# Evacuations and a triangular inverse dealt anew among ScalarE, VectorE and GpSimd in a chunked delta-rule scan

## The chip, the core and the metric

One core of a Trainium2 chip runs the whole program. The metric is the device time of one execution in microseconds. Engines are written as in the profile: PE (TensorE matmul), PEld (its weight loads), DVE (VectorE), ACT (ScalarE), POOL (GpSimd) and SP (the queue that issues most DMAs).

## The reference, cut to what matters

One inference step of a two-layer trunk of width 1024 over 128 prompt tokens and 512 latent tokens. Layer 0 mixes tokens with a gated MLP, layer 1 with RWKV-7: two scans, forward and backward, over a 64x64 state for each of 16 heads. The edit is in the scans.

```python
def _wkv_scan(s0, r, decay, k, v, kk, a, reverse):
    def step(s, inp):
        r_t, w_t, k_t, v_t, kk_t, a_t = inp
        sa = jnp.einsum('bhij,bhj->bhi', s, -kk_t)
        s = (s * w_t[:, :, None, :]
             + sa[..., None] * (kk_t * a_t)[:, :, None, :]
             + v_t[..., None] * k_t[:, :, None, :])
        return s, jnp.einsum('bhij,bhj->bhi', s, r_t)
    ...
for d in range(N_DIR):
    ...
    s_fin, y_d = _wkv_scan(s0[:, d], r, decay, k_d, v, kk, a, reverse=(d == 1))
    y = y + y_d
```

Prompt and latent tokens run through the same weights; the latent scan starts from a cached state, the prompt scan from zero, and the prompt's final states are an output.

## The kernel before

The scans are done in chunks of 64 tokens: 2 chunks of prompt and 8 of latents, ten in all. Within a chunk the delta rule needs the inverse of a unit triangular 64x64 matrix for each head. So the work has four parts, for eight groups g = 0 to 7 (four pairs of head pairs, p = g // 2, in two directions, d = g % 2):

- The inverse of a group (`inv_start`, `inv_prep`, `inv_sub`). A DVE transpose (L836) lays out the two 32x32 diagonal blocks of all chunks and heads as LA, 128 partitions with one small matrix each. Then come 31 steps of forward substitution, each an outer product (L843) and a subtraction (L845) on LX. Step s works on rows s+1 to 31 and columns 0 to s. In the kernel before, POOL does columns 0 to 10 (`CS = 11`), and DVE the columns from 11 on in the steps s = 11 to 30, in instructions that `spread` deals out over the slots of the schedule. The inverse of group 0 runs earlier, under the projections, and wholly on POOL.
- `merges`: two DVE transposes of LX (L978, L981), 80 small matmuls with their ACT evacuations (L1002, L1019) that build the off-diagonal blocks, and four copies of diagonal blocks into TT, the finished inverse (L1024, DVE).
- `Front`: for each of ten units of a group, three products into PSUM. `p1` gives the score matrices B (a masked half, L927 on DVE, and a plain half, L929 on ACT), `wt` gives WT (L944, DVE), `wp` multiplies by TT and gives WP (L958, ACT).
- `chain`: ten dependent steps a group, one for each chunk, both head pairs (ti) in each. `part1` multiplies the state in RZ by WP into PSUM za; both heads' halves are evacuated, negated, into RZ (head 0 by ACT at L1066, head 1 by DVE at L1067). `part2` adds the products with B into PSUM sy; the state rows are evacuated with a scale into the next chunk's RZ (head 0 by DVE at L1088, head 1 by ACT at L1086), the output rows into Y (L1091 on ACT for d = 0, added on DVE at L1093 for d = 1). PSUM holds one za, and one sy for each ti, so the next step's sy has to wait for these evacuations.

Two tables say where in the program each part is written: `FA` gives the slots of the units of a group (20 slots a group, two a step), `MG` and `MGS` those of the merges. The inverse of group j is started in slot 7 of group j-2, and merged in group j-1. The order of instructions on each engine is then set when the program is built: a list scheduler with its own costs puts each instruction into its engine's queue as soon as its inputs are ready by those costs, chain instructions first (`tc.high_priority(30)`). On the chip each queue runs strictly in that order. SBUF space for the four pieces LA, LX and the two transposes (`piece`) is used again from inverse to inverse.

```python
def inv_start(d):
    LA, LX = piece(), piece()
    inv_prep(d, LA, LX)
    for s in range(31):
        inv_sub(nc.gpsimd, inv[:, 4416:4648], LA, LX, s, 0, min(s + 1, CS))
    return LX, [lambda s=s: inv_sub(vec, inv[:, 4648:4880], LA, LX, s, CS, s + 1) for s in range(CS, 31)]
```

Of the kernel before, what the change touches and what calls it, by code (L numbers as in the profile page):

```python
# [7 lines left out]
F32 = mybir.dt.float32  # L8
# [7 lines left out]
P = 128  # L16
# [12 lines left out]
def tile_trunk(ctx: ExitStack, tc: tile.TileContext, a: dict):  # L29
# [782 lines left out]

    def rwkv_core(dr, PC, bon, nn, ATs, go):
        with ExitStack() as es:
            CS = 11
            NR, NK = 10, 4

            xw = Pool(hctx, "cxw", {"w": 1}, side="right")
# [41 lines left out]
            while not go:  # L860
                yield
            xk = Pool(hctx, "cx", {"x": 1})
            cp = Pool(es, "cc", {"T": 4, "K": NK, "B": 8, "WT": 3, "WP": 7, "R": NR, "TT": 2, "b": 9})
            ea, ef = ExitStack(), ExitStack()
            cl = ap = None

# [20 lines left out]
                vec.memset(x, 0.0)  # L887
            turn_ = [0]

            mT = cp.tile([P, 2, 2, 64], F32, "WT", "mT")  # L890
            vec.memset(mT, 1.0)
            for d in range(2):
                for h in range(2):
                    a0 = 64 * h
                    vec.tensor_copy(mT[a0:a0 + 64, d, 1 - h], masks[a0:a0 + 64, 1 - d, 0])

            class Front:
                def __init__(self, g):
# [19 lines left out]
                def p1(self, i):  # L918
                    u = self.buf[self.units[i]]
                    R, Tt = u[0], u[3]  # L920
                    B = cp.tile([P, 2, 4, 64], F32, "B", "B")
                    ps = pf.tile([P, 2, 4, 64], F32, "p", "p1")
                    for e in range(2):
                        for x, j in ((R[:, :, e], 3 * e), (ident.rearrange("p (h c) -> p h c", h=2), 1 + e)):
                            for m in range(2):
                                pe.matmul(ps[64 * m:64 * m + 64, :, j], Tt[:, 2 * e + m], x, start=True, stop=True)  # L926
                    vec.tensor_tensor(out=B[:, :, 0:4:3], in0=ps[:, :, 0:4:3], op=ALU.mult,  # L927
                                      in1=masks[:, self.d, 1].unsqueeze(1).unsqueeze(1).to_broadcast([P, 2, 2, 64]))
                    act.copy(B[:, :, 1:3], ps[:, :, 1:3])  # L929
                    u[4] = B  # L930


# [15 lines left out]
                def wp(self, i):  # L948
                    ti, q = self.units[i]
                    u = self.buf[ti, q]  # L950
                    W = u[3]
                    ps = pf.tile([P, 2, 4, 64], F32, "p", "wpps")
                    for e in range(2):
                        for j in range(2):
                            pe.matmul(ps[64 * j:64 * j + 64, :, e], W[:, e, j],  # L955
                                      TTs[self.d][:, 10 * ti + 2 * q + e], start=True, stop=True)
                    WP = cp.tile([P, 2, 2, 64], F32, "WP", "WP")
                    act.copy(WP, ps[:, :, 0:2])  # L958
                    u[2] = WP

            def load_AT(g):
# [5 lines left out]
            def inv_start(d):  # L967
                LA, LX = piece(), piece()
                inv_prep(d, LA, LX)
                for s in range(31):  # L970
                    inv_sub(nc.gpsimd, inv[:, 4416:4648], LA, LX, s, 0, min(s + 1, CS))
                return LX, [lambda s=s: inv_sub(vec, inv[:, 4648:4880], LA, LX, s, CS, s + 1) for s in range(CS, 31)]

            def merges(d, LX):
                AT, TT = ATs[d], TTs[d]
# [45 lines left out]

                def diag(h, b):
                    p0 = 64 * h + 32 * b
                    vec.tensor_copy(TT[p0:p0 + 32, :, h, 32 * b:32 * b + 32],  # L1024
                                    XDT[p0:p0 + 32].rearrange("p t u -> p u t")[:, U0[d]:U0[d] + 20])

                for ti in range(2):
# [22 lines left out]
            def part1(d, fr, RZ, c, ti, upd):  # L1050
                q, e = divmod(c, 2)
                with HP():
                    R, _, WP, _, _ = fr.buf[ti, q]
                    za = pp.tile([P, 8, 64], F32, "za", "za")[:, 0]
                    sy = pp.tile([P, 8, 64], F32, f"sy{ti}", "sy")[:, 0:2]
                    for h in range(2):
                        a0 = 64 * h
                        pe.matmul(za[a0:a0 + 64], WP[:, h, e], RZ[:, ti, h, c], start=True, stop=True)  # L1058
                    s0, y0 = 64 * (1 - e), 64 * e
                    for h in range(2):  # L1060
                        a0 = 64 * h
                        if upd:
                            pe.matmul(sy[s0:s0 + 64, h], ident[:, a0:a0 + 64], RZ[:, ti, h, c],
                                      start=h == 0, stop=False)
                        pe.matmul(sy[y0:y0 + 64, h], R[:, h, e], RZ[:, ti, h, c], start=h == 0, stop=False)
                    act.activation(out=RZ[0:64, ti, 0, c], in_=za[0:64], func=AF.Copy, scale=-1.0)  # L1066
                    vec.tensor_scalar(out=RZ[64:128, ti, 1, c], in0=za[64:128], scalar1=-1.0, scalar2=None, op0=ALU.mult)  # L1067
                return sy

            def part2(d, p, fr, RZ, c, nxt, ti, sy, Y, so):  # L1070
                q, e = divmod(c, 2)
                with HP():
                    B = fr.buf[ti, q][4]
                    s0, y0 = 64 * (1 - e), 64 * e
                    upd = nxt is not None or c < 2
                    for h in range(2):
                        if upd:
                            pe.matmul(sy[s0:s0 + 64, h], B[:, h, 1 + e], RZ[:, ti, h, c], start=False, stop=h == 1)  # L1078
                        pe.matmul(sy[y0:y0 + 64, h], B[:, h, 3 * e], RZ[:, ti, h, c], start=False, stop=h == 1)  # L1079
                    if upd:  # L1080
                        for h in range(2):
                            a0 = 64 * h
                            dst = RZ[a0:a0 + 64, ti, h, nxt] if nxt is not None else so[a0:a0 + 64, ti]
                            pc = PC[s0:s0 + 64, d, 2 * p + ti, h, q:q + 1]
                            if h:
                                act.activation(out=dst, in_=sy[s0:s0 + 64, h], func=AF.Copy, scale=pc)  # L1086
                            else:
                                vec.tensor_scalar(out=dst, in0=sy[s0:s0 + 64, h], scalar1=pc, scalar2=None, op0=ALU.mult)  # L1088
                    Yc = Y[y0:y0 + 64, q]
                    if d == 0:  # L1090
                        act.copy(Yc, sy[y0:y0 + 64])  # L1091
                    else:
                        vec.tensor_tensor(out=Yc, in0=Yc, in1=sy[y0:y0 + 64], op=ALU.add)  # L1093
                    if nxt is None and c < 2 and ti:
                        nc.sync.dma_start(out=a["sT"][:, 2 * p:2 * p + 2, d], in_=so)
# [123 lines left out]

            class Tail:  # L1220
                def __init__(self):
                    self.rings = {"x": (3, []), "r": (3, []), "o": (3, []), "s": (2, [])}
                    self.x, self.stored = None, []
                    self.first = self.early()

# [200 lines left out]
            FA = (-8, -6, -4, -2, 0, 2, 4, 6, 8, 10)  # L1426
            MG = (4, 5, 7, 8, 9, 10, 11)
            LAP = 7
            DV0, DV1 = (7, 24)
            ADA = (0, 1, 3, 7, 9, 10, 11, 14, 15, 19)  # L1430
            AG = 2
            FW = (1, 3, 1, 1, 1, 1, 1, 1, 1, 1, 1, 1, 1, 1, 1, 1, 1, 1, 1, 1)
# [5 lines left out]
            GE = vec  # L1438
            STQ = nc.scalar
            posts = []  # L1440
            MGS = {0: (5, 6, 8, 9, 10, 11, 12), 1: (6, 7, 9, 10, 11, 11, 12)}
            ZL = 4
            DVI = (0, 5)
            sched = {}

            def at(k, f):
                sched.setdefault(k, []).append(f)

            def spread(fs, a, b):
                for i, f in enumerate(fs):  # L1450
                    at(a + i * (b - a) // len(fs), f)

            spread(lx[1][1], *DVI)
            for g in range(8):
                for i in range(10):
                    k, f = 20 * g + FA[i], fr[g]
                    for k0, x in ((k - 6, f.load), (k - 3, f.p1), (k - 2, f.wt), (k, f.wp)):
                        at(max(k0, -1), lambda i=i, x=x: x(i))
            for x in sched.pop(-1):
                x()  # L1460
            for j in range(2, 8):
                k0 = 20 * (j - 2) + (ZL if j == 2 else 0)

                def start(j=j, k0=k0):
                    lx.append(inv_start(j % 2))
                    spread(lx[j][1], k0 + DV0, min(k0 + DV1, 20 * j - 20 + MGS.get(j - 1, MG)[0]))

                at(k0 + LAP - 4, lambda j=j: load_AT(j))
                at(k0 + LAP, start)
# [14 lines left out]
            for g in range(8):  # L1484
# [4 lines left out]
                if g < 7:  # L1489
                    ms = {}  # L1490

                    def merge(g=g):
                        if g not in ms:
                            ms[g] = merges((g + 1) % 2, lx[g + 1][0])
                        adv(ms[g])

                    for x in MGS.get(g, MG):
                        at(20 * g + x, merge)
# [205 lines left out]
```

## Time and profile before

| | |
|---|---|
| median of 3 runs | 2150.9 us (2149.31 to 2154.84) |
| profiled execution | 2151.84 us, span 2150.1 us |
| PE busy | 2001.1 us, 93% |
| DVE busy | 1175.1 us, 55% |
| ACT busy | 753.8 us, 35% |
| POOL busy | 383.3 us, 18% |
| the scans | from about 1075 to 1610 us of the span |

The spans of PE are modelled and its matmuls are pipelined, so its 93% is not a measure of how full it is. In the lines of groups, the last column is the time for which an engine sat idle just before an instruction of the group, and what ended it. In a table of stretches, the columns behind an engine's busy time are the granted TensorE clock, the DMA share and GB/s.

### The profile page before, as it was taken

Reading aid. Unit: us, or ns where it says so; the run is one execution under the profiler, and the core shown is the slowest. Engines: PE = TensorE matmul, PEld = TensorE weight load, DVE = VectorE, ACT = ScalarE, POOL = GpSimd, SP = SyncE. Lnnn points to the kernel's source line nnn. Section 1 sums busy time; section 2 is a strip of 40 time slices with the busy share of each in tenths; the row PEclk is TensorE's granted clock in tenths of the full one; section 3 lists DMA queues with packets and bytes.
Section 4 is the critical chain, followed back from the end, with each engine's and each line's share of the span. In section 5 each row is a group of like instructions: output and inputs, shape, how many; then the busy total and the mean of one; then the engine's idle time right before and its main releaser. Section 6 shows DMA issues by size and latency. Waiting matters only on the chain.

```text
span 2150.1 us, 43942 instructions
## 1 busy us (share of the span) xinstructions
PE 2001.1 (93%) x18294; PEld 1763.8 (82%) x18294; DVE 1175.1 (55%) x2231; ACT 753.8 (35%) x1505; POOL 383.3 (18%) x681
## 2 busy tenths in 40 slices
PE   6999999999999798989888998888998999999997
PEld 5767889999999587878677776766765899999997
DVE  5435643333333796767688877757455633333334
ACT  5323531313132264655444433432422522222231
POOL 0000000000000301588367435414000000000000
PEclk9999999999999799989889998987999999999998
DMA  8554352222222033666442344442440222222221
GB/s 279 203 193 161 114 177 70 79 75 73 79 71 79 19 119 126 191 197 198 140 117 74 114 142 123 141 130 66 135 131 30 79 79 78 70 79 73 75 69 50
DMA packets 149670, 241.78 MB, mean 112 GB/s; under 512 B 28128, under 2 KB 98400, under 8 KB 149344
## 3 DMA queue, kind: packets, MB, share of 16 engines
q1 hardware_dynamic: 149040, 238.52, 34.8%
q8 instruction: 144, 2.36, 0.5%
q14 instruction: 54, 0.44, 0.1%
q10 hardware_dynamic: 432, 0.46, 0.1%
HBM read 197.63 MB, written 38.67 MB: 110 GB/s over the span
## 4 chain that ended last, share of the span: by engine, by line
PE 76%; POOL 8%; DVE 8%; issue 3%; ACT 3%; DMA 2%; SPq 0%; POOLq 0%; DVEq 0%; ACTq 0%
PE fmps L114 46%; PE zps L310 5%; POOL inv L845 3%; POOL inv L843 3%; PE vps L754 2%; PE p L926 2%; PE rps L114 2%; PE wops L1271 2%; PE wops L1371 1%; PE adaps L122 1%; PE adaps L1193 1%; PE sy L1078 1%; PE wtps L942 1%; PE l1ps L507 1%; PE wpps L955 1%
## 5 line engine op out<-in xcount | busy, mean ns | idle before, releaser
L114 PE MATMUL fmps<-ahi,whi 128*128 128x256 f32 (+1 forms) x2272 | 534.6, 310 | 4.9 <-ACT ahi L100 3.1
L114 PE MATMUL fmps<-alo,whi 128*128 128x256 f32 (+1 forms) x2272 | 533.7, 309 | 1.3 <-DVE alo L101 1.3
L114 PE MATMUL fmps<-ahi,wlo 128*128 128x256 f32 (+1 forms) x2272 | 533.8, 309 | 0.0
L114 PEld LDWEIGHTS fmps<-ahi,whi 128*128 128x128 f32 x2272 | 414.4, 188 | 11.0 <-ACT ahi L100 5.5
L114 PEld LDWEIGHTS fmps<-alo,whi 128*128 128x128 f32 x2272 | 415.1, 188 | 2.1 <-DVE alo L101 1.8
L114 PEld LDWEIGHTS fmps<-ahi,wlo 128*128 128x128 f32 x2272 | 415.2, 188 | 1.0 <-issue 0.8
L88 ACT CAST whi<-wraw 128x1024 fp32r<-128x1024 f32 x174 | 182.5, 1050 | 633.5 <-PE fmps L114 538.2
L89 DVE TENSOR_TENSOR wlo<-wraw,whi 128x1024 fp32r<-128x1024 f32 x174 | 216.3, 1244 | 273.2 <-ACT whi L88 273.0
L283 DVE SCALAR_TENSOR_TENSOR x<-fmps,mod,x 128x128 f32<-128x128 f32 (+2 forms) x153 | 74.5, 527 | 305.4 <-PE fmps L114 305.4
L491 POOL TENSOR_TENSOR xx<-h 128x254 f32<-128x254 f32 (+1 forms) x16 | 12.0, 751 | 724.7 <-DVE h L210 710.0
L843 POOL TENSOR_TENSOR inv<-inv 128x220 f32<-128x220 f32 (+29 forms) x217 | 100.3, 462 | 165.7 <-DVE inv L836 149.2
L845 POOL TENSOR_TENSOR inv<-inv 128x220 f32<-128x220 f32 (+29 forms) x217 | 101.0, 466 | 17.0
L1078 PE MATMUL sy<-RZ,B 128*64 128x64 f32 x576 | 79.8, 244 | 14.1 <-ACT RZ L1066 7.7
L1079 PE MATMUL sy<-RZ,B 128*64 128x64 f32 x640 | 87.6, 244 | 1.1 <-DVE RZ L1067 0.8
L926 PE MATMUL p<-cst,Tt 128*64 128x128 f32 x640 | 87.4, 291 | 0.0
L926 PE MATMUL p<-R,Tt 128*64 128x128 f32 x640 | 85.8, 297 | 0.2 <-DMA R<-dR 0.2
L1078 PEld LDWEIGHTS sy<-RZ,B 128*64 128x64 f32 x576 | 56.3, 146 | 35.6 <-ACT RZ L1066 14.8
L1058 PE MATMUL za<-RZ,WP 128*64 128x64 f32 x640 | 67.1, 245 | 16.0 <-DVE RZ L1088 8.1
L1066 ACT ACTIVATE RZ<-za 64x64 f32<-64x64 f32 x160 | 34.8, 217 | 126.3 <-PE za L1058 69.2
L955 PE MATMUL wpps<-TT,WT 128*64 128x128 f32 x640 | 68.2, 290 | 11.4 <-ACT B L929 7.0
L101 DVE TENSOR_TENSOR alo<-rsq,ahi 128x640 fp32r<-128x640 f32 (+2 forms) x69 | 53.6, 777 | 45.6 <-ACT ahi L100 45.3
L942 PE MATMUL wtps<-cst,K 128*64 128x64 f32 x640 | 70.2, 235 | 8.9 <-DVE WT L944 4.5
(282 smaller groups left out, 3690.2 us busy)
## 6 DMA issues: line engine op xcount, KB each, us to landing
wraw<-w SPq DMA_DIRECT2D x126, 512.0 KB, 3.5
wraw<-ada SPq DMA_DIRECT2D x64, 512.0 KB, 5.0
adaw<-adac SPq DMA_DIRECT2D x32, 512.0 KB, 3.7
dT<-IT SPq DMA_DIRECT2D x16, 640.0 KB, 3.9
Tt<-dT SPq DMA_DIRECT2D x80, 128.0 KB, 2.7
wraw<-w_in SPq DMA_DIRECT2D x16, 512.0 KB, 5.1
dR<-KR SPq DMA_DIRECT2D x16, 320.0 KB, 3.3
dT<-KR SPq DMA_DIRECT2D x16, 320.0 KB, 3.0
```

The source lines that it names most:

```text
L88: act.copy(hi[:, :n], r[:, :n])
L89: vec.tensor_tensor(out=lo[:, :n], in0=r[:, :n], in1=hi[:, :n], op=ALU.subtract)
L114: pe.matmul(ps[:, PS0 + t0:PS0 + t1], w, x[:, t0:t1], start=start, stop=stop)
L283: vec.scalar_tensor_tensor(out=X[n][:, t0:t1], in0=ps[:, t0 - r[0]:t1 - r[0]], scalar=mod[l][:, which, n, g:g + 1], in1=X[n][:, t0:t1], op ...
L310: pe.matmul(pss[i], x[:, i * P:(i + 1) * P], w[:, kq * 512:(kq + 1) * 512], start=(k == 0 and j == 0), stop=(k == KT - 1 and j == 2))
L843: eng.tensor_tensor(out=tv, in0=LA[:, s + 1:32, s:s + 1].to_broadcast([P, n, m]), in1=LX[:, s:s + 1, c0:c1].to_broadcast([P, n, m]), op=AL ...
L845: eng.tensor_tensor(out=LX[:, s + 1:32, c0:c1], in0=LX[:, s + 1:32, c0:c1], in1=tv, op=ALU.subtract)
L926: pe.matmul(ps[64 * m:64 * m + 64, :, j], Tt[:, 2 * e + m], x, start=True, stop=True)
L942: pe.matmul(ps[a0:a0 + 64, e, j], K[:, h, e], x, start=True, stop=True)
L955: pe.matmul(ps[64 * j:64 * j + 64, :, e], W[:, e, j], TTs[self.d][:, 10 * ti + 2 * q + e], start=True, stop=True)
L1078: pe.matmul(sy[s0:s0 + 64, h], B[:, h, 1 + e], RZ[:, ti, h, c], start=False, stop=h == 1)
L1079: pe.matmul(sy[y0:y0 + 64, h], B[:, h, 3 * e], RZ[:, ti, h, c], start=False, stop=h == 1)
```

## The change

It deals the work of the scans out anew, and moves the program's slots for group 1.

- POOL does all columns of the inverse (`inv_sub(..., 0, s + 1)`); the DVE pieces and their `spread` go.
- The four diagonal copies of a merge go from DVE to POOL (L1027).
- ACT does all four evacuations that the chain waits for: both halves of za (L1071) and both of the state (L1089).
- DVE does all those of the products: B in one instruction of 512 columns with a mask mB that holds ones in the plain half (L932), WT (L947), WP (L961), and Y for both directions (L1092, L1094).
- The slots of group 1's units come from tables of their own (L1, P1, W1, F1), later than before, its merges move from slots 5 to 12 to slots 11 to 17, and inverse 2 starts three slots later (`ZL`).
- SBUF: mB is new, mT gets a place of its own, and the pools b and the tail's ring o lose a buffer each.

```diff
-                    vec.tensor_tensor(out=B[:, :, 0:4:3], in0=ps[:, :, 0:4:3], op=ALU.mult,
-                                      in1=masks[:, self.d, 1].unsqueeze(1).unsqueeze(1).to_broadcast([P, 2, 2, 64]))
-                    act.copy(B[:, :, 1:3], ps[:, :, 1:3])
+                    vec.tensor_tensor(out=B, in0=ps, in1=mB[:, self.d].unsqueeze(1).to_broadcast([P, 2, 4, 64]), op=ALU.mult)
...
-                    act.copy(WP, ps[:, :, 0:2])
+                    vec.tensor_copy(WP, ps[:, :, 0:2])
...
-                    inv_sub(nc.gpsimd, inv[:, 4416:4648], LA, LX, s, 0, min(s + 1, CS))
-                return LX, [lambda s=s: inv_sub(vec, inv[:, 4648:4880], LA, LX, s, CS, s + 1) for s in range(CS, 31)]
+                    inv_sub(nc.gpsimd, inv[:, 4416:4672], LA, LX, s, 0, s + 1)
+                return LX
...
-                    vec.tensor_copy(TT[p0:p0 + 32, :, h, 32 * b:32 * b + 32],
+                    nc.gpsimd.tensor_copy(TT[p0:p0 + 32, :, h, 32 * b:32 * b + 32],
...
-                    act.activation(out=RZ[0:64, ti, 0, c], in_=za[0:64], func=AF.Copy, scale=-1.0)
-                    vec.tensor_scalar(out=RZ[64:128, ti, 1, c], in0=za[64:128], scalar1=-1.0, scalar2=None, op0=ALU.mult)
+                    for h in range(2):
+                        a0 = 64 * h
+                        act.activation(out=RZ[a0:a0 + 64, ti, h, c], in_=za[a0:a0 + 64], func=AF.Copy, scale=-1.0)
...
-                            if h:
-                                act.activation(out=dst, in_=sy[s0:s0 + 64, h], func=AF.Copy, scale=pc)
-                            else:
-                                vec.tensor_scalar(out=dst, in0=sy[s0:s0 + 64, h], scalar1=pc, scalar2=None, op0=ALU.mult)
+                            act.activation(out=dst, in_=sy[s0:s0 + 64, h], func=AF.Copy, scale=pc)
...
-                        act.copy(Yc, sy[y0:y0 + 64])
+                        vec.tensor_copy(Yc, sy[y0:y0 + 64])
...
-            MGS = {0: (5, 6, 8, 9, 10, 11, 12), 1: (6, 7, 9, 10, 11, 11, 12)}
-            ZL = 4
+            MGS = {0: (11, 12, 13, 14, 15, 16, 17), 1: (6, 7, 9, 10, 11, 11, 12)}
+            ZL = 7
```

Three places show what this does to the queues. The first is DVE's in the first chain, around the transpose that closes inverse 1 (L978 before, L981 in the changed kernel, each reading the LX that POOL fills). Before:

```order
L843 TENSOR_TENSOR inv<-inv 128x20
L1088 TENSOR_SCALAR RZ<-sy,PC 64x64
L845 TENSOR_TENSOR inv<-inv 128x20
L927 TENSOR_TENSOR B<-p_10319,cst 128x2x2x64
L978 STREAM_TRANSPOSE inv<-inv 128x1024
L944 TENSOR_TENSOR WT<-wtps,mT 128x256
L1067 TENSOR_SCALAR RZ<-za 64x64
L981 STREAM_TRANSPOSE inv<-inv 128x1024
```

Now:

```order
L1092 COPY Y<-sy 64x128
L961 COPY WP<-wpps 128x256
L932 TENSOR_TENSOR B<-p_9931,mB 128x512
L947 TENSOR_TENSOR WT<-wtps,mT 128x256
L932 TENSOR_TENSOR B<-p_9959,mB 128x512
L961 COPY WP<-wpps 128x256
L947 TENSOR_TENSOR WT<-wtps,mT 128x256
L981 STREAM_TRANSPOSE inv<-inv 128x1024
L932 TENSOR_TENSOR B<-p_10058,mB 128x512
L651 TENSOR_TENSOR KR<-kk,Pt 128x5x128
L961 COPY WP<-wpps 128x256
L1092 COPY Y<-sy 64x128 x2
```

The transpose stood behind three steps of the chain (six L1067 in the queue ahead of it); it stands behind one step now (two Y copies), and the second step's Y copies behind it.

The second is DVE's queue in the chain of group 3, around the transpose that closes inverse 5. Before:

```order
L1088 TENSOR_SCALAR RZ<-sy,PC 64x64
L843 TENSOR_TENSOR inv<-inv 128x38
L1093 TENSOR_TENSOR Y<-Y,sy 64x128
L845 TENSOR_TENSOR inv<-inv 128x2x19
L1093 TENSOR_TENSOR Y<-Y,sy 64x128
L843 TENSOR_TENSOR inv<-inv 128x20
L944 TENSOR_TENSOR WT<-wtps,mT 128x256
L845 TENSOR_TENSOR inv<-inv 128x20
L978 STREAM_TRANSPOSE inv<-inv 128x1024
L927 TENSOR_TENSOR B<-p_13604,cst 128x2x2x64
L981 STREAM_TRANSPOSE inv<-inv 128x1024
L1067 TENSOR_SCALAR RZ<-za 64x64
```

Now:

```order
L1094 TENSOR_TENSOR Y<-Y,sy 64x128 x2
L947 TENSOR_TENSOR WT<-wtps,mT 128x256
L981 STREAM_TRANSPOSE inv<-inv 128x1024
L932 TENSOR_TENSOR B<-p_13399,mB 128x512
L1198 STREAM_TRANSPOSE adat<-adaps 128x512
L961 COPY WP<-wpps 128x256
L1199 TENSOR_TENSOR mod_88<-adat,adab 128x32
L984 STREAM_TRANSPOSE inv<-inv 128x1024
L1094 TENSOR_TENSOR Y<-Y,sy 64x128 x2
```

It stood five steps behind the transpose that opens the inverse (L836), and stands four behind it now (L835); the next step's Y waits behind it, and no RZ does.

The third is POOL's queue between inverses 4 and 5. Before:

```order
L843 TENSOR_TENSOR inv<-inv 128x22
L845 TENSOR_TENSOR inv<-inv 128x2x11
L843 TENSOR_TENSOR inv<-inv 128x11
L845 TENSOR_TENSOR inv<-inv 128x11
L837 MEMSET inv 128x1024
L838 MEMSET inv 128x32
L843 TENSOR_TENSOR inv<-inv 128x31
L845 TENSOR_TENSOR inv<-inv 128x31
```

Now:

```order
L842 TENSOR_TENSOR inv<-inv 128x60
L844 TENSOR_TENSOR inv<-inv 128x2x30
L842 TENSOR_TENSOR inv<-inv 128x31
L844 TENSOR_TENSOR inv<-inv 128x31
L1027 COPY TT_9559<-inv 32x20x32 x4
L836 MEMSET inv 128x1024
L837 MEMSET inv 128x32
L842 TENSOR_TENSOR inv<-inv 128x31
```

The last steps of an inverse are as wide as its first ones now (all columns), and four copies into TT stand between one inverse and the memset of the next.

More of the change, by code (lines that the diff above doesn't have):

```diff
@@ L814, in rwkv_core @@
         with ExitStack() as es:
-            CS = 11
             NR, NK = 10, 4
@@ L862, in rwkv_core @@
             xk = Pool(hctx, "cx", {"x": 1})
-            cp = Pool(es, "cc", {"T": 4, "K": NK, "B": 8, "WT": 3, "WP": 7, "R": NR, "TT": 2, "b": 9})
+            cp = Pool(es, "cc", {"T": 4, "K": NK, "B": 8, "WT": 2, "WP": 7, "R": NR, "TT": 2, "mB": 1, "mT": 1, "b": 8})
             ea, ef = ExitStack(), ExitStack()
@@ L888, in rwkv_core @@
             turn_ = [0]
-            mT = cp.tile([P, 2, 2, 64], F32, "WT", "mT")
+            mT = cp.tile([P, 2, 2, 64], F32, "mT", "mT")
             vec.memset(mT, 1.0)
@@ L895, in rwkv_core @@
                     vec.tensor_copy(mT[a0:a0 + 64, d, 1 - h], masks[a0:a0 + 64, 1 - d, 0])
+            mB = cp.tile([P, 2, 4, 64], F32, "mB", "mB")
+            vec.memset(mB, 1.0)
+            for d in range(2):
+                for j in (0, 3):
+                    vec.tensor_copy(mB[:, d, j], masks[:, d, 1])
             class Front:
@@ L1221, in __init__ @@
                 def __init__(self):
-                    self.rings = {"x": (3, []), "r": (3, []), "o": (3, []), "s": (2, [])}
+                    self.rings = {"x": (3, []), "r": (3, []), "o": (2, []), "s": (2, [])}
                     self.x, self.stored = None, []
@@ L1428, in rwkv_core @@
             LAP = 7
-            DV0, DV1 = (7, 24)
             ADA = (0, 1, 3, 7, 9, 10, 11, 14, 15, 19)
@@ L1440, in rwkv_core @@
             posts = []
-            MGS = {0: (5, 6, 8, 9, 10, 11, 12), 1: (6, 7, 9, 10, 11, 11, 12)}
-            ZL = 4
-            DVI = (0, 5)
+            MGS = {0: (11, 12, 13, 14, 15, 16, 17), 1: (6, 7, 9, 10, 11, 11, 12)}
+            L1 = (13, 14, 15, 16, 20, 20, 21, 22, 23, 25)
+            P1 = (16, 16, 17, 18, 21, 21, 21, 23, 25, 27)
+            W1 = (19, 19, 20, 21, 22, 24, 22, 24, 26, 28)
+            F1 = (19, 19, 20, 21, 22, 24, 24, 26, 28, 30)
+            ZL = 7
             sched = {}
@@ L1447, in at @@
                 sched.setdefault(k, []).append(f)
[L1449 to L1453, printed above, removed]
             for g in range(8):
@@ L1456, in rwkv_core @@
                     k, f = 20 * g + FA[i], fr[g]
-                    for k0, x in ((k - 6, f.load), (k - 3, f.p1), (k - 2, f.wt), (k, f.wp)):
+                    for k0, x in zip((L1[i], P1[i], W1[i], F1[i]) if g == 1 else (k - 6, k - 3, k - 2, k),
+                                     (f.load, f.p1, f.wt, f.wp)):
                         at(max(k0, -1), lambda i=i, x=x: x(i))
@@ L1462, in rwkv_core, with start @@
                 k0 = 20 * (j - 2) + (ZL if j == 2 else 0)
-                def start(j=j, k0=k0):
+                def start(j=j):
                     lx.append(inv_start(j % 2))
-                    spread(lx[j][1], k0 + DV0, min(k0 + DV1, 20 * j - 20 + MGS.get(j - 1, MG)[0]))
                 at(k0 + LAP - 4, lambda j=j: load_AT(j))
@@ L1493, in merge @@
                         if g not in ms:
-                            ms[g] = merges((g + 1) % 2, lx[g + 1][0])
+                            ms[g] = merges((g + 1) % 2, lx[g + 1])
                         adv(ms[g])
```

## The prediction

> **What bounds the kernel now.** I read the page for where the engines stand, then the chain of waits over the scans alone (1060 to 1620 us), then the instructions that start and end a triangular inverse, then the chain's pace between them.
>
> ```profile
> span 2150.1 us, 43942 instructions
> ...
> DVE  5435643333333796767688877757455633333334
> POOL 0000000000000301588367435414000000000000
> ...
> by line: POOL inv L845 10.7%; POOL inv L843 10.3%; PE p L926 7.3%; PE wops L1271 6.5%; issue 6.4%; PE adaps L1193 4.2%; PE sy L1078 4.1%; PE wtps L942 3.9%; PE wpps L955 3.6%; PE za L1058 3.6%; PE sy L1063 2.7%; PE tps L1012 2.6%; PE gps L9
> ```
>
> The scans are slices 20 to 29 of the page (53.75 us each). DVE is 70 to 80% busy in their first half, the highest of the whole program, and yet 21% of the path through the stretch (10.7 + 10.3, 118 of 560 us) is POOL's two lines of the inverse. So POOL's inverse is already on the path; the vector queue says how. "Opening" below is the transpose that hands an inverse its matrix (L836; L835 after), "closing" the first transpose of its result (L978; L981 after).
>
> ```profile
> 1074.78 2.07 DVE L836 STREAM_TRANSPOSE inv<-AT 128x1024 f32<-128x1024 f32 x1
> ...
> 1117.39 1.95 DVE L978 STREAM_TRANSPOSE inv<-inv 128x1024 f32<-128x1024 f32 x1 [2.21 <-POOL inv L845]
> 1369.55 2.09 DVE L836 STREAM_TRANSPOSE inv<-AT 128x1024 f32<-128x1024 f32 x1 [2.16 <-ACT AT L834]
> 1403.15 1.91 DVE L978 STREAM_TRANSPOSE inv<-inv 128x1024 f32<-128x1024 f32 x1 [5.70 <-POOL inv L845]
> 1446.05 2.11 DVE L836 STREAM_TRANSPOSE inv<-AT 128x1024 f32<-128x1024 f32 x1
> 1480.08 1.90 DVE L978 STREAM_TRANSPOSE inv<-inv 128x1024 f32<-128x1024 f32 x1 [6.17 <-POOL inv L845]
> ...
> PE za L1058 <- DVE RZ L1088: 8.1, 2, 7.8
> PE wpps L955 <- ACT B L929: 7.0, 1, 7.0
> ```
>
> The closing transpose stands in DVE's queue at a fixed place. If POOL is not done when DVE gets there, everything queued behind it waits, and PE's two longest waits (7.8 and 7.0 us) are the two 6 us waits of DVE passed on. Opening to closing is 33.6 us for inverse 6 and 34.0 for inverse 7. What the chain does meanwhile, and between a closing and the next opening, is counted by ACT's half of the first evacuation (L1066, two a step), in stretches cut at those transposes:
>
> ```profile
> core 0: us, ACT busy (x), PEclk, DMA share, GB/s
> ...
> 1160.00:1208.00 48.00, 3.85 (x18) 0.96 0.28 78
> 1208.00:1222.00 14.00, 1.29 (x6) 1.00 0.54 162
> 1264.00:1295.00 31.00, 2.18 (x10) 1.00 0.54 172
> 1295.00:1329.00 34.00, 2.18 (x10) 0.85 0.44 126
> 1331.00:1369.00 38.00, 2.61 (x12) 0.96 0.46 142
> 1369.00:1403.00 34.00, 1.74 (x8) 0.89 0.40 123
> 1405.00:1446.00 41.00, 3.06 (x14) 0.95 0.49 145
> 1446.00:1480.00 34.00, 1.74 (x8) 0.65 0.20 56
> 1482.00:1610.00 128.00, 8.92 (x42) 0.98 0.42 128
> ```
>
> Outside the inverses (1208, 1264, 1331, 1405) 21 steps take 124 us, 5.9 us a step. Inverse 3 covers nine steps, inverse 5 five, inverses 6 and 7 four each: 34 us for four steps is where time is lost.
>
> **The change, part by part.** *POOL takes the whole inverse.*
>
> ```profile
> 1297.70:1329.50 31.80, 26.89 (x62) 0.84 0.42 125
> 1448.20:1480.10 31.90, 26.96 (x62) 0.64 0.18 51
> 1076.80:1117.40 40.60, 34.73 (x62) 0.86 0.45 132
> ...
> L845 POOL TENSOR_TENSOR inv<-inv 128x198 f32<-128x198 f32 x7 | 4.0, 573 | 0.5
> ...
> L845 POOL TENSOR_TENSOR inv<-inv 128x11 f32<-128x11 f32 x7 | 1.5, 211 | 0.5
> ...
> L843 DVE TENSOR_TENSOR inv<-inv 128x20 f32<-128x20 f32 (+9 forms) x140 | 53.9, 385 | 3.5
> L1024 DVE COPY TT<-inv 32x640 f32<-32x640 f32 x32 | 24.4, 763 | 0.7
> ...
> 1066.12 1.53 POOL L722 TENSOR_TENSOR k<-k,ta 128x640 f32<-128x640 f32 x1
> ```
>
> The two shapes give a line: (573 - 211)/187 = 1.94 ns an element over 0.19 us. Now 62 instructions work on 2 x 3,916 elements (the sum over s of (31-s) x min(s+1, 11)): 11.8 + 15.2 = 27.0 us, and the windows say 26.9 and 27.0. Afterwards the same 62 work on 2 x 5,456: 11.8 + 21.2 = 33.0 us. With the gaps of now (31.9 - 27.0 = 4.9) that is 38 us, and 40.3 from opening to end with the 2.2 us that lie ahead of POOL's first instruction now. The 40 DVE instructions of each inverse go.
>
> The Trainium skill (GPSIMD Engine Reference, Engine selection) has two-input elementwise work about twice as slow there as on VectorE. By that page the moved instructions, 2 x 53.9/7 = 15 us an inverse on DVE, would cost 31 us on POOL and not 6. The trace agrees only for whole instructions; here columns are added to instructions that run anyway, so their fixed 0.19 us is not paid again.
>
> *The four diagonal copies go to POOL*, ahead of the next inverse's memset, and in inverses 1 and 2 ahead of its first instruction. No row shows such a copy there: DVE's 0.76 us is one end, POOL's two-input 128x640 of 1.53 us the other; I take 1.1, between, 4.5 us for four.
>
> *The chain's evacuations.*
>
> ```profile
> L1086 ACT ACTIVATE RZ<-sy,PC 64x64 f32<-64x64 f32 x128 | 37.9, 307 | 49.8 <-DVE RZ L1088 47.8
> L1067 DVE TENSOR_SCALAR RZ<-za 64x64 f32<-64x64 f32 x160 | 36.4, 227 | 38.4 <-ACT RZ L1066 19.0 <-PE sy L1065 14.6 <-PE wtps L942 1.0
> L1066 ACT ACTIVATE RZ<-za 64x64 f32<-64x64 f32 x160 | 34.8, 217 | 126.3 <-PE za L1058 69.2 <-PE sy L1065 51.1 <-PE wtps L942 1.9
> L1088 DVE TENSOR_SCALAR RZ<-sy,PC 64x64 f32<-64x64 f32 x128 | 33.7, 279 | 21.5 <-PE sy L1079 16.7 <-PE wpps L955 2.6
> L944 DVE TENSOR_TENSOR WT<-wtps,mT 128x256 f32<-128x256 f32 x80 | 33.7, 421 | 13.0 <-PE wtps L942 11.4
> L927 DVE TENSOR_TENSOR B<-p,cst 128x256 f32<-128x256 f32 x80 | 33.6, 420 | 11.5 <-PE p L926 10.1
> L958 ACT COPY WP<-wpps 128x256 f32<-128x256 f32 x80 | 29.7, 371 | 52.9 <-PE wpps L955 39.5 <-PE wtps L942 5.4 <-PE sy L1079 4.3
> L929 ACT COPY B<-p 128x256 f32<-128x256 f32 x80 | 29.5, 369 | 53.5 <-DVE B L927 52.9
> L1093 DVE TENSOR_TENSOR Y<-Y,sy 64x128 f32<-64x128 f32 x79 | 21.6, 284 | 7.8 <-ACT RZ L1086 5.0 <-ACT inv L1086 0.6 <-PE sy L1079 0.2
> L1091 ACT COPY Y<-sy 64x128 f32<-64x128 f32 x80 | 20.1, 260 | 2.2 <-PE sy L1079 1.0
> ```
>
> ACT gives up 29.7 + 29.5 + 20.1 = 79 us and takes 160 x 0.217 + 144 x 0.307 = 79: even. DVE gives up 36.4 + 33.7 here, 24.4 of diagonals and twice 53.9 of inverse, 202 us; it takes 80 copies like L944's (34), 80 Y copies like L1093's (23), and 256 more columns in 80 masks, at (421 - 284)/128 = 1.07 ns each 22 us. Net 123 us off DVE, 1.5 us a step. The two halves of an evacuation run one after the other now, on two engines: ACT waits 47.8 us for DVE, DVE 19.0 for ACT. That is 66.8 us over 80 steps, 0.8 a step, and on one engine it goes. What a step saves is not shown by any row; its ends are nothing (PE's own work sets the pace) and 1.5 us (DVE's queue sets it). I take 0.7, near the 0.8 of those handovers: 5.2 us a step. In the last stretch (21 steps, 128 us, with the tail's matmuls between) I take 0.5.
>
> *The order.* Of the two evacuations of a step, Y is on DVE for every group. It frees the one bank that the next step's sy needs, so a closing transpose that waits stops the chain within about a step. Between opening and closing, in Y's of the queue (two a step), the changed order has 1, 7, 4, 4, 4, 4 and 3.5 steps for inverses 1 to 7; before, 3, 6.5, 9, 6, 5, 4 and 3.5. Between a closing and the next opening it has 2, 0, 7, 8, 7 and 7 steps, and 21.5 behind the last. So more steps lie outside a longer inverse.
>
> The sum by position, from the opening of inverse 1:
> - Opening 1 at 1074.8 + 1.1: mB's memset and four copies are new ahead of it, five short DVE instructions taken at L1067's 0.23. POOL copies four diagonals (until 1080.4), then 38 us and 4, half of the 7.8 that this inverse loses now beside DVE's work (34.7 - 26.9), since the inverse's part of that work goes: closing 1 at 1122.4.
> - The closing's transpose (1.95) and two steps (10.4): opening 2 at 1135. Four diagonals and 38: closing 2 at 1178, since the seven steps between, 36 us, fit.
> - Opening 3 follows that transpose and two evacuations, at 1182; 40.3 and four diagonals inside: closing 3 at 1226.5, with 14 steps done. Before, the chain has 19 by 1208.
> - From there 7, 8, 7 and 7 steps outside, 29 x 5.2 = 150.8, and four inverses: 40.3 twice, and 42 for the two that run beside the post steps of a finished pair (an estimate, far under the 7.7 that DVE's work beside it adds to inverse 1). Closing 7 at 1226.5 + 150.8 + 164.6 = 1542, 62 us behind 1480.1.
> - The 21 steps after it: -10.5.
>
> Sum +51 us on the profiled execution's own 2151.84, which stands 0.9 above the median 2150.9: 2202 on the median. With s saved per step everywhere the sum is 82 - 50 s; s = 0 gives 2233, s = 1.28 (the best stretch, 14/3 = 4.7 us a step) 2169. The pool sizes that change (WT, b, the tail's ring o) cost nothing: mT leaves WT with the two that W used, and the ring serves the tail, whose DVE work is hidden by 0.98 clock of matmuls; a stall there would be 1 or 2 us.
>
> **Rivals.**
> 1. *Faster: DVE's queue, not POOL, sets the pace.* For it: DVE is the busiest engine of that stretch and loses 1.5 us a step. It decides from s = 1.64 (4.3 us a step); at s = 1.9 the sum is -13, 2138. Against: the last stretch has no inverse on DVE and full clock and still takes 6.1 a step, and inverses 1 to 3 follow each other on POOL until 1226.5 whatever a step takes. 0.14 faster, 0.06 within the bound.
> 2. *Slower still: PE's clock falls in the new waits.* The granted clock is 1.00 in 1208 to 1222 and 0.65 in 1446 to 1480, where DVE waits 6.2 us. Six closings would wait 10 us or more. If the matmuls behind each run slow, the 0.7 us are lost again and the tail gains nothing: 2233, and 5 to 10 more for the waits' ends. 0.22. The Trainium skill (TensorE: Matmul & The Clock Gate, What's actually happening) has the array at half rate after an idle window of some 3.4 us until it has been busy for one; by that rule each such wait costs about one window at half rate, an estimate of 6 x 1.7 = 10 us, 2212. The trace's low clock in the stretch with the wait agrees.
> 3. *The waits hide nothing new*, because an inverse is covered anyway: then 34 + 6 us need 7.7 steps under them, and the order has four. It would give about 2100; it is in the 0.14.
>
> **How the numbers follow.** The forecast's case (s from 0.3 to 1.3) has 0.58, rival 2 0.22, rival 1 0.20 with its part within the bound. 2202 is the likeliest's. The range goes from 2150, which leaves out most of rival 1, to 2238, which leaves out the worst of rival 2. About 0.3% (6.5 us) is what a measurement here can tell from nothing: faster 0.14, same 0.06, slower 0.80. The slower cases' own range is 2169 to 2238.
>
> **What would show it.** L842 and L844 on POOL at 33 us an inverse, 38 us from first to last. Closing transposes (L981) with 10 to 25 us of idle time before them, released by POOL, for inverses 1 and 3 to 7; the diagonal copies (L1027) near 1.1 us; L1071 and L1089 with no wait on DVE; 5.2 us a step outside the inverses; the chain's last step 50 us later. Wrong if those idle times are under 5 us, or if a step takes 4.2.

## The result: 3.0% slower, and the profile after

The changed kernel takes 2218.0 us (median of 4 runs, 2211.6 to 2220.4) against 2152.0 for the kernel before beside it: a ratio of 1.0302, 95% interval 1.0276 to 1.0328. The prediction was 2202, between 2150 and 2238. Differences between kernels below come from such ratios, since the kernel before has its own median on each chip (2149 to 2154).

The page's first line and the rows of the 40 slices, after (a slice is 55.4 us now):

```profile
span 2216.8 us, 43728 instructions
...
DVE  5434642333335977766543632533543733333334
POOL 0000000000001103885778445346000000000000
```

The scans are slices 19 to 30 (counted from 0). DVE's digits there, 6 to 8 in the first half before, are 2 to 6 now, and the program became slower: DVE was not short of time. What it does instead is the last column of the seven transposes that close inverses 1 to 7 (start, us, engine, line, what, then the idle time before it and what ended it):

```profile
1120.93 1.90 DVE L981 STREAM_TRANSPOSE inv<-inv 128x1024 f32<-128x1024 f32 x1 [22.49 <-POOL inv L844]
...
1174.66 1.93 DVE L981 STREAM_TRANSPOSE inv<-inv 128x1024 f32<-128x1024 f32 x1 [8.35 <-POOL inv L844]
...
1221.67 1.90 DVE L981 STREAM_TRANSPOSE inv<-inv 128x1024 f32<-128x1024 f32 x1 [19.38 <-POOL inv L844]
...
1296.39 1.25 DVE L984 STREAM_TRANSPOSE inv<-inv 128x1024 f32<-128x1024 f32 x1 [20.64 <-POOL inv L844]
1384.17 1.90 DVE L981 STREAM_TRANSPOSE inv<-inv 128x1024 f32<-128x1024 f32 x1 [10.49 <-POOL inv L844]
...
1461.76 1.90 DVE L981 STREAM_TRANSPOSE inv<-inv 128x1024 f32<-128x1024 f32 x1 [15.65 <-POOL inv L844]
...
1542.17 1.90 DVE L981 STREAM_TRANSPOSE inv<-inv 128x1024 f32<-128x1024 f32 x1 [15.91 <-POOL inv L844]
```

(For inverse 4 the transpose of L984 came first.) That is 112.9 us of DVE standing still (16.5 before). The view of waits shows them again on PE (us in total, times, longest: the long ones are three on B and one in each other row), and PE's row of the stretches shows what they come to, from 1060 us to the last evacuation of za, before and after:

```profile
PE p L931 <- DVE B L932: 49.9, 3, 22.1
PE wtps L945 <- DVE WT L947: 15.9, 1, 15.9
PE ytps L1160 <- DVE inv L1150: 12.4, 1, 12.4
PE sy L1066 <- DVE Y L1092: 12.2, 3, 11.6
PE gps L997 <- DVE inv L981: 8.9, 1, 8.9
```

```profile
1060.00:1610.00 550.00, 484.97 (x8087) 0.91 0.40 118
```

```profile
1060.00:1677.00 617.00, 491.20 (x8082) 0.87 0.35 105
```

PE idles 125.8 us there instead of 65.0. In the records of its matmuls, seven gaps of over 5 us hold 98.8 us of it (two with 14.8 before), and all shorter ones 27.0 (50.2 before). So the 67 us are +84 in long waits, -23 in short ones and +6 of PE's busy time for the same matmuls. These three numbers are what the experiments take apart; "long" and "short" below mean PE's gaps over and under 5 us in this stretch.

### The profile page after: what moved, and what is told of

Its sections match the earlier page's. It is cut to its first block, busy times and chain, and to the rows that moved or that the text cites. A ratio compares the mean times of both kernels' runs of the same rounds, so it can differ in the third digit from the quotient of the medians.

```text
span 2216.8 us, 43728 instructions
## 1 busy us (share of the span) xinstructions
PE 2006.0 (90%) x18294; PEld 1769.5 (80%) x18294; DVE 1050.0 (47%) x1780; ACT 755.1 (34%) x1569; POOL 453.6 (20%) x713
## 5 line engine op out<-in xcount | busy, mean ns | idle before, releaser
L1071 ACT ACTIVATE RZ<-za 64x64 f32<-64x64 f32 x320 | 69.6, 218 | 285.1 <-PE sy L1068 203.0
L842 POOL TENSOR_TENSOR inv<-inv 128x31 f32<-128x31 f32 (+15 forms) x217 | 109.4, 504 | 150.2 <-DVE inv L835 133.7
L931 PE MATMUL p<-R,Tt 128*64 128x128 f32 x640 | 83.7, 297 | 50.2 <-DVE B L932 49.9
L844 POOL TENSOR_TENSOR inv<-inv 128x31 f32<-128x31 f32 (+15 forms) x217 | 119.0, 548 | 16.9
L931 PEld LDWEIGHTS p<-R,Tt 128*64 128x64 f32 x640 | 51.6, 147 | 55.6 <-DVE B L932 50.5
L1089 ACT ACTIVATE RZ<-sy,PC 64x64 f32<-64x64 f32 x256 | 71.2, 305 | 71.2 <-PE sy L1083 64.6
L945 PE MATMUL wtps<-cst,K 128*64 128x64 f32 x640 | 70.2, 235 | 20.3 <-DVE WT L947 15.9
L932 DVE TENSOR_TENSOR B<-p,mB 128x512 f32<-128x512 f32 x80 | 55.0, 688 | 50.3 <-PE p L931 47.2
L1083 PE MATMUL sy<-RZ,B 128*64 128x64 f32 x640 | 75.9, 240 | 0.2 <-ACT RZ L1071 0.2
L1066 PE MATMUL sy<-RZ,cst 128*64 128x64 f32 x576 | 60.7, 238 | 17.1 <-DVE Y L1092 12.2
L100 ACT CAST ahi<-rsq 128x640 fp32r<-128x640 f32 (+2 forms) x69 | 47.5, 688 | 82.0 <-DVE rsq L435 81.7
```

Of the source, the lines that this page charges most:

```text
L842: eng.tensor_tensor(out=tv, in0=LA[:, s + 1:32, s:s + 1].to_broadcast([P, n, m]), in1=LX[:, s:s + 1, c0:c1].to_broadcast([P, n, m]), op=AL ...
L844: eng.tensor_tensor(out=LX[:, s + 1:32, c0:c1], in0=LX[:, s + 1:32, c0:c1], in1=tv, op=ALU.subtract)
L945: pe.matmul(ps[a0:a0 + 64, e, j], K[:, h, e], x, start=True, stop=True)
L1071: act.activation(out=RZ[a0:a0 + 64, ti, h, c], in_=za[a0:a0 + 64], func=AF.Copy, scale=-1.0)
```

## The experiments

The theory (A): the loss is a queue position. POOL's inverse is 5 us longer, the closing transpose stands only a few steps behind the opening in DVE's queue, and everything behind it waits. Rivals: (B) the new evacuations cost; (C) POOL's result itself comes too late, wherever the transposes stand.

**The inverse alone put back, and the inverse alone moved.** The first is the changed kernel with the pieces of the inverse dealt as before, the second the kernel before with the same lines the other way round:

```diff
-                    inv_sub(nc.gpsimd, inv[:, 4416:4672], LA, LX, s, 0, s + 1)
-                return LX
+                    inv_sub(nc.gpsimd, inv[:, 4416:4648], LA, LX, s, 0, min(s + 1, CS))
+                return LX, [lambda s=s: inv_sub(vec, inv[:, 4648:4880], LA, LX, s, CS, s + 1) for s in range(CS, 31)]
```

> The changed kernel with the inverse alone dealt as before (POOL columns 0 to 10, DVE the rest); the evacuations, diagonal copies and slots stay changed. Theory A (the loss is DVE's in-order wait at the closing transposes for the longer POOL inverse): POOL needs about 32 us again, closings stand 4, 6, 6, 8.5, 4, 4, 3 steps behind the openings, idle time of DVE before them falls from 113 us to 30 to 50, and the time to 2150 to 2175. Rival B (the new evacuations are what costs: ACT one after the other, B of 512 columns late for PE): 2190 or more.

> The kernel before with the inverse alone moved whole to POOL; evacuations, diagonal copies and slots as before. Theory A: closings stand 1.5, 5, 5, 4, 4.5, 3.5, 3.5 steps behind the openings, DVE waits 80 to 110 us before them, 2200 to 2235. Rival B (evacuations): under 2175.

Put back: 2150.7 us, 0.9992 of before (0.9978 to 1.0006). Moved alone: 2227.6 us, 1.0350 (1.0327 to 1.0373). The closing transposes' groups, first of the kernel with the inverse put back, then of the one with the inverse alone moved:

```profile
L982 DVE STREAM_TRANSPOSE inv<-inv 128x1024 f32<-128x1024 f32 x8 | 15.4, 1930 | 22.7 <-POOL inv L845 22.6
```

```profile
L977 DVE STREAM_TRANSPOSE inv<-inv 128x1024 f32<-128x1024 f32 x8 | 15.2, 1898 | 86.0 <-POOL inv L844 82.4 <-PE gps L993 3.6
L980 DVE STREAM_TRANSPOSE inv<-inv 128x1024 f32<-128x1024 f32 x8 | 9.9, 1242 | 38.5 <-POOL inv L844 38.4
```

The whole inverse costs 3.1 to 3.5% with either set of evacuations, more than the whole change. Its waits come with it: 121 us released by POOL (more than the 80 to 110 expected), 23 without it (fewer than the 30 to 50). Rival B falls.

Two things come together in these waits, and no run separates them. POOL needs 5 us more, and DVE, rid of its own pieces of the inverse, reaches the closing earlier. For inverse 3 the queue has five steps between opening and closing in the second kernel, where the kernel before has nine. For inverses 6 and 7 the place is almost the same (3.5 steps, 4 and 3.5 before), and their waits still grow from 5.7 and 6.2 us to 19.9 and 16.6.

**The tie.** This edit touches the closing transposes alone; the program's scheduler then orders everything else around them. One element of the latest Y is copied into each transpose's output first; the transpose then has to stand behind that Y in the queue (the copies take 0.13 us each).

```diff
+                if y is not None:
+                    vec.tensor_copy(Q1[y[0]:y[0] + 1, 0, 0:1], y[1][0:1, 0, 0:1])
                 vec.transpose(out=Q1, in_=LX.rearrange("p r c -> p c r"))
...
+                    last[0] = (y0, Yc)
...
-                            ms[g] = merges((g + 1) % 2, lx[g + 1])
+                            ms[g] = merges((g + 1) % 2, lx[g + 1], last[0])
```

> The changed kernel, with one element of the latest Y written into each closing transpose's output first, so that the closings of inverses 1 to 7 stand 6, 10, 12, 9, 9, 8 and 7 steps behind the openings in DVE's queue instead of 1, 7, 4, 4, 4, 4, 3.5; the inverse stays whole on POOL. Theory A (a queue position, not POOL's length): DVE's idle time before closings falls from 113 us to under 20, PE's gaps of over 5 us from 98.8 to under 25, 2120 to 2150. Rival C (the chain needs the inverse's result and POOL is simply too long): the wait moves on to the matmuls that read TT, 2190 or more.

> The kernel before with the same tie: closings 3, 8.5, 12.5, 8.5, 8.5, 7.5, 7.5 steps behind the openings instead of 3, 6.5, 9, 6, 5, 4, 3.5. Theory A: the two 6 us waits and their 14.8 us of PE gaps go, 2135 to 2148. Rival C: 2150 or more.

The changed kernel with the tie: 2148.1 us, 0.9976 of before (0.9962 to 0.9990), 3.2% under the same kernel without it. POOL's inverse is as long as ever. Its closing transposes:

```profile
L985 DVE STREAM_TRANSPOSE inv<-inv 128x1024 f32<-128x1024 f32 x8 | 15.5, 1944 | 11.4 <-POOL inv L844 11.3
```

Inverses 3 to 7, with their readers seven to twelve steps behind, wait under 2 us together: theory A. Rival C is left with the first two inverses, which follow each other on POOL. DVE waits 9.6 us at the closing of inverse 2, ten steps behind, and 14.5 us in front of the transpose that opens inverse 2, until 1123.1 us, when POOL is at the end of inverse 1. On PE two long gaps (22.8 us) are left, which are followed up below.

The kernel before with the tie: 2126.6 us, 0.9876 (0.9852 to 0.9900). That is 27 us, where 4 to 17 were expected. Its long gaps (14.8) are gone; the short ones fell from 50.2 to 45.5, and PE's busy time in the stretch from 485.0 to 478.5:

```profile
1060.00:1584.00 524.00, 478.51 (x8077) 0.94 0.42 123
```

The stretch is 26 us shorter: 14.8 + 4.7 of gaps and 6.5 of PE's busy time. The matmuls ran faster in it: the granted clock of the stretch is 0.94, against 0.91 before.

**The evacuations alone, and with the tie.** The kernel before with the evacuations of the change, inverse, diagonal copies and slots as before; then the same with the tie; then, without the evacuations, the kernel before with the whole inverse and the tie.

```diff
-                    vec.tensor_scalar(out=RZ[64:128, ti, 1, c], in0=za[64:128], scalar1=-1.0, scalar2=None, op0=ALU.mult)
+                    for h in range(2):
+                        a0 = 64 * h
+                        act.activation(out=RZ[a0:a0 + 64, ti, h, c], in_=za[a0:a0 + 64], func=AF.Copy, scale=-1.0)
...
-                    act.copy(WP, ps[:, :, 0:2])
+                    vec.tensor_copy(WP, ps[:, :, 0:2])
```

> The kernel before with the chain's and the products' evacuations alone dealt anew (ACT and DVE); inverse, diagonal copies and group 1's slots as before. If the evacuations save what the changed kernel's PE gaps under 5 us show (27.0 us there against 50.2, 0.3 us a step), these gaps are 25 to 35 us here; closings stand 4, 8, 12, 6, 4, 4, 3 steps behind the openings, so inverses 5 to 7 wait 5 to 8 us each: 2135 to 2155. Rival B (the evacuations cost): 2160 or more. Rival D (they save 0.7 us a step, as predicted): under 2125.

> The same with the tie: closings 4, 8, 15, 8, 9, 8, 7 steps behind. If the evacuations save 0.3 us a step whatever the closings do: 2100 to 2115, 12 to 25 under the tied kernel before (2126.6). Rival E (without the waits PE is the pace and the evacuations save nothing): 2120 to 2135.

> The kernel before with the whole inverse on POOL and the tie: closings 3.5, 8, 12, 9.5, 9, 8, 7.5 steps behind. Theory A: 2125 to 2150, against 2227.6 without the tie, with waits left at inverse 1 and 2, which follow each other on POOL. Rival C (POOL's length delays TT itself): 2180 or more.

| kernel | us | of before, 95% interval | long gaps | short gaps |
|---|---|---|---|---|
| evacuations alone | 2142.1 | 0.9952 (0.9937 to 0.9966) | 13.7 | 42.0 |
| tie alone | 2126.6 | 0.9876 (0.9852 to 0.9900) | 0 | 45.5 |
| evacuations and tie | 2123.5 | 0.9870 (0.9854 to 0.9885) | 0 | 39.8 |
| whole inverse and tie | 2130.6 | 0.9903 (0.9889 to 0.9918) | 14.4 | 31.2 |

The evacuations save 10 us by themselves. That is inside the expected time (and rival D, under 2125, falls), but the short gaps are 42.0 where 25 to 35 were expected. So the 23 us that the change takes out of them are mostly not the evacuations' (8 of 50). The row with the whole inverse points to the rest: with DVE's 40 instructions per inverse gone, they fall from 45.5 to 31.2. But one long gap of 14.4 us takes their place, so what this relief is worth by itself no run shows. With the tie the evacuations save nothing that the intervals tell: not the 12 to 25 us expected for 0.3 a step, and 2123.5 lies in rival E's range. The one long gap of the last row is inverse 1's: its closing stands 3.5 steps behind, and DVE waits 13.7 us there.

**What is left in the tied changed kernel.** First the slots of group 1 as before, then also the diagonal copies on DVE again:

```diff
-            MGS = {0: (11, 12, 13, 14, 15, 16, 17), 1: (6, 7, 9, 10, 11, 11, 12)}
+            MGS = {0: (5, 6, 8, 9, 10, 11, 12), 1: (6, 7, 9, 10, 11, 11, 12)}
...
-            ZL = 7
+            ZL = 4
...
-                    for k0, x in zip((L1[i], P1[i], W1[i], F1[i]) if g == 1 else (k - 6, k - 3, k - 2, k),
+                    for k0, x in zip((k - 6, k - 3, k - 2, k),
...
-                    nc.gpsimd.tensor_copy(TT[p0:p0 + 32, :, h, 32 * b:32 * b + 32],
+                    vec.tensor_copy(TT[p0:p0 + 32, :, h, 32 * b:32 * b + 32],
```

> The tied changed kernel with group 1's slots as before (unit tables, merge slots and start of inverse 2). The tied one had 22.8 us of PE gaps left, at 1183 and 1214 us, in group 1's chain, where TT of groups 1 and 2 came late. If the later slots of group 1 make these, they go and the time is 2120 to 2135; if the two inverses one behind the other on POOL make them, they stay and it is 2140 to 2160.

> The tied changed kernel with group 1's slots as before and the diagonal copies on DVE again. In the trace of the one with POOL's copies, those of inverse 2 stand in POOL's queue inside inverse 3, and PE waits 23.9 us for the last of them at 1213 us. If that is the queue position of the copies: this gap goes, some 7 to 15 us of inverse 1's wait stay, 2115 to 2128. If the copies only show what the merge's transposes or matmuls are late for: 2138 or more.

With the slots alone the time is 2145.5 us, 0.9979 (0.9968 to 0.9990): they were not it. PE has long gaps of 7.2 us (at 1127) and 23.9 us (at 1213) now. For the second the trace names what ends it, and POOL's own timeline says why that is so late:

```profile
1213.27 0.48 PE L958 MATMUL wpps<-TT,WT 128*64 128x128 f32 x2 [23.93 <-POOL TT L1033]
```

```profile
1207.10 1.25 POOL L1033 COPY TT<-inv 32x640 f32<-32x640 f32 x1
1208.32 0.28 POOL L842 TENSOR_TENSOR inv<-inv 128x60 f32<-128x60 f32 x1
1208.66 1.24 POOL L1033 COPY TT<-inv 32x640 f32<-32x640 f32 x1
...
1211.98 1.24 POOL L1033 COPY TT<-inv 32x640 f32<-32x640 f32 x1
1213.30 0.25 POOL L844 TENSOR_TENSOR inv<-inv 128x31 f32<-128x31 f32 x1
```

The four copies of inverse 2 stand between the last instructions of inverse 3 (the 128x60 and 128x31 ones), 34 us behind the transposes they read. It is the mechanism of A again, in another queue. With the copies on DVE the gap is gone: 2121.7 us, 0.9871 (0.9854 to 0.9888). This is the whole inverse, the new evacuations and the tie, 4.2% under the changed kernel and 1.3% under the kernel before. Evacuations and tie with the inverse dealt as before had 2123.5: once its readers stand late enough, the whole inverse on POOL costs nothing that the intervals tell. That settles rival C. It has the fastest median, but its interval overlaps those of the tied kernel before and of evacuations and tie.

**The two small parts without the tie.** Diagonal copies alone back on DVE, and group 1's slots alone as before, by the lines above:

> The changed kernel with the diagonal copies alone on DVE again. Closings 1, 7, 3, 4, 4, 4, 3.5 steps behind the openings, as in the changed kernel but for one. Inverse 1 starts on POOL some 5 us earlier (four copies of 1.3 us no longer ahead of it), so its closing comes 5 us earlier; DVE takes 24 us back, which its waits hide: 2208 to 2222. Under 2195 if POOL's copies cost more than that; over 2225 if DVE's queue is short of time.

> The changed kernel with group 1's slots alone as before (closings 1, 5, 5, 4, 4, 4, 3.5 steps behind). Inverse 2's wait grows from 8.4 us to 12 to 18, inverse 3's falls by about as much: 2210 to 2226. If the later slots are what delays chains 1 and 2 (18 us later than before at the start of chain 1): under 2205.

Copies back: 2211.0 us, 1.0287 (1.0271 to 1.0303), as expected; its interval overlaps that of the changed kernel, so without the tie the copies' place can't be told from nothing. Slots back: 2226.7 us, 1.0355 (1.0338 to 1.0373), just over the 2226 expected. The changed slots save some 11 us: inverse 2's wait is 12.9 us without them and 8.4 with them; inverse 3's is 19.4 in both, where a fall was expected.

**A last wait.** The fastest kernel, with the merge of inverse 1 later, so that its closing stands five steps behind. (Its last parts come after the first unit of group 1 has read TT, so that unit multiplies by a TT that is not finished; the amount of work is the same.)

```diff
-            MGS = {0: (5, 6, 8, 9, 10, 11, 12), 1: (6, 7, 9, 10, 11, 11, 12)}
+            MGS = {0: (9, 10, 11, 12, 12, 13, 13), 1: (6, 7, 9, 10, 11, 11, 12)}
```

> The tied changed kernel with group 1's units and inverse 2 as before, diagonal copies on DVE, and the merge of inverse 1 in slots 9 to 13 instead of 5 to 12, so that its closing stands 5 steps behind the opening instead of 3. The last long wait of the tied kernels (11.9 us of DVE, 8.3 of PE at 1123 us) shrinks to under 3: 2110 to 2120. If inverse 1's result is then late for chain 1 instead: 2120 to 2130.

2125.5 us, 0.9875 (0.9847 to 0.9903): nothing gained. DVE no longer waits at the closing, but 11 us at the next transpose of its queue, the opening of inverse 2, whose output still belongs to inverse 1. Neither expectation named that place, though DVE had waited 14.5 us there in the tied changed kernel.

```profile
1124.86 1.90 DVE L835 STREAM_TRANSPOSE inv<-AT 128x1024 f32<-128x1024 f32 x1 [11.04 <-POOL inv L842]
```

## Why the prediction held, and where it was off

**POOL's inverse**: 33.0 us busy and 38 from first to last were forecast. POOL's rows for inverse 5, and for inverse 3 with the four diagonal copies inside:

```profile
1347.10:1384.20 37.10, 32.24 (x62) 0.86 0.31 97
...
1179.40:1221.70 42.30, 37.30 (x66) 0.82 0.25 68
```

32.2 and 37.1: right, with 5.2 us more work than the 27.0 of before. The estimate by the Trainium skill (GPSIMD Engine Reference, Engine selection) was 31 more; these columns, added to instructions that already ran, didn't follow it. A copy takes 1.37 us on the mean of 32 (1.1 was taken):

```profile
L1027 POOL COPY TT<-inv 32x640 f32<-32x640 f32 x32 | 43.9, 1373 | 23.9 <-DVE inv L984 9.8 <-PE wpps L958 6.9 <-DVE inv L981 6.1
```

The same page of the Trainium skill calls one-input work there "roughly line-rate"; this copy took 0.76 us on DVE, so the trace does not agree for this shape.

**The waits**: forecast were 10 to 25 us for inverses 1 and 3 to 7; measured 22.5, 19.4, 20.6, 10.5, 15.7 and 15.9. Inverse 2, for which no wait was forecast ("since the seven steps between, 36 us, fit"), waits 8.4. The sum had closings 1, 2, 3 and 7 at 1122.4, 1178, 1226.5 and 1542; they are at 1120.9, 1174.7, 1221.7 and 1542.2. The way from DVE to the chain was drawn too narrowly. Not the bank of sy and the Y copies alone pass the wait on (one case in seven, 11.6 us): PE's own queue stops at whichever product next needs a result of DVE's, three times the score products, which wait for B.

**Outside the inverses**, 5.2 us a step were forecast and the pace stayed at 5.8 (5.9 before). The count of ACT's first evacuation (L1071, four a step), in the stretches between closings and openings from closing 3 on, and behind the last:

```profile
1224.00:1255.50 31.50, 6.09 (x28) 0.95 0.36 105
...
1298.00:1344.80 46.80, 6.53 (x30) 0.92 0.44 134
...
1384.20:1422.60 38.40, 5.66 (x26) 0.91 0.45 143
...
1461.80:1502.80 41.00, 5.22 (x24) 0.91 0.43 125
...
1542.20:1677.00 134.80, 17.76 (x82) 0.97 0.40 121
```

The first four are 27 steps in 157.7 us, 5.84 a step; the sum had 29 steps at 5.2, 150.8 us. That it still met closing 7 is luck: at this pace 29 steps would have been 169 us, but two of them stood inside the inverses, four openings to closings took 160.5 and not 164.6, and closing 3 came 5 us earlier. The last row is the term that was mis-sized: 134.8 us, where the sum had the 130 of before less 10.5. Those 15 us are the whole distance between forecast and result. PE's share suggests why no evacuation could save there, before and after:

```profile
1480.00:1610.00 130.00, 125.25 (x1790) 95.24 (x1790) 74.03 (x223) 45.73 (x157) 1.32 (x2) 0.97 0.41 126
```

```profile
1542.20:1677.00 134.80, 128.09 (x1774) 97.11 (x1775) 69.25 (x179) 46.48 (x174) 6.40 (x5) 0.97 0.40 121
```

PE (the first number behind the length) is 95 to 96% busy. Why the stretch became even 5 us longer is not isolated: from closing 7 to the last evacuation of za the kernel with the inverse alone moved takes 130.8 us, the one with the evacuations alone 133.2.

The step of the prediction that failed is "I take 0.7, near the 0.8 of those handovers". The handovers did go, as forecast: neither line of ACT waits for DVE now. But the waits did not.

```profile
L1089 ACT ACTIVATE RZ<-sy,PC 64x64 f32<-64x64 f32 x256 | 71.2, 305 | 71.2 <-PE sy L1083 64.6 <-PE wtps L945 3.0 <-PE p L931 0.3
L1071 ACT ACTIVATE RZ<-za 64x64 f32<-64x64 f32 x320 | 69.6, 218 | 285.1 <-PE sy L1068 203.0 <-PE za L1061 71.9 <-PE sy L1083 3.9
```

Where ACT stood 47.8 us for DVE before, it stands for PE: the 66.8 us of handovers were for the most part not on the path. Evacuations alone save 10 us in 80 steps, 0.13 a step. The short gaps that went with DVE's part of the inverse are 14 us more, 0.18. With both, 0.3, the prediction's own 82 - 50 s gives +67, the measured loss; but that they meet is no proof, since the pace between the inverses shows only 0.06 a step and the last stretch none.

**Rivals.** The first (DVE's queue sets the pace) is out: DVE is less busy and the program slower. The second (PE's clock) is real but small. PE's rows in pieces of 2 us after the 22 us wait (the columns behind the busy time are the granted clock, the DMA share and GB/s):

```profile
1123.40:1125.40 2.00, 1.94 (x14) 0.50 0.00 0
1125.40:1127.40 2.00, 1.90 (x26) 0.50 0.62 161
1127.40:1129.40 2.00, 2.00 (x51) 0.80 0.89 249
1129.40:1131.40 2.00, 1.01 (x17) 1.00 0.26 66
```

Half clock lasts two stretches and two fifths of the third, 4.8 us. Behind the wait that ends at 1224.2 us it is one stretch and half of the next, 3.0 us:

```profile
1224.20:1226.20 2.00, 2.00 (x24) 0.50 0.00 0
1226.20:1228.20 2.00, 1.92 (x33) 0.75 0.10 25
```

The Trainium skill's rule (TensorE: Matmul & The Clock Gate, What's actually happening) has half rate after an idle window until the array has been busy for one of some 3.4 us; the trace agrees, with 3.0 and 4.8 us in these two places. The prediction's estimate by it was 10 us; PE's busy time in the scans grew by 6.2. The third rival (an inverse is covered anyway) is what the tie makes of it: it needs some seven steps of cover, as the prediction reckoned (inverse 7, seven steps behind in the tied changed kernel, waits 1.7 us), and the queue gave four.

Still open: why the tied kernels don't gain from the relief of DVE and the evacuations together. All of them without POOL's copies lie between 2121.7 and 2130.6, at a PE that is busy for 479 to 483 us of 517 to 528. With the whole inverse, a wait of 8 to 14 us on inverse 1 stays on PE; the one attempt to move it only changed its place.

## What to carry to other kernels

Before moving work to an idle engine, find the instruction that reads its result and count what lies between the two in the reader's queue: here 5 us more on POOL, and a DVE that came to its reader earlier, became 16 us of standstill on the mean of seven inverses (2 before), and 67 us in all. A busy share that falls while the time grows was the sign of it. The cheap cure is to move the reader, not the work: a copy of one element that makes it stand behind a later instruction was worth 27 us before the change and 70 after it.

## What the runs showed of the hardware

Waits of PE came with slower matmuls behind them. Taking 14.8 us of long gaps out of the kernel before took 6.5 us off PE's busy time for the same matmuls as well. With the new evacuations, 13.7 us of gaps went and 3.1 us of busy time (484.3 to 481.3), so the price is not a fixed one. A 32x640 copy between differently ordered views took 1.24 to 1.37 us on POOL, 0.76 on DVE.
